# A hybrid decoder step on one core: the inverse's corner blocks brought back by TensorE identity columns, its inputs loaded by two transfers per batch, and four smaller edits

## The chip, the core and the metric

One core of a Trainium2 chip runs the whole kernel. The metric is the device time of one execution in microseconds (us); the time of a kernel is the median of its runs. The kernel before takes 2013.07 us (three runs, 2012.75 to 2020.41).

## What is computed

One layer of a hybrid decoder for 256 prompt tokens and 8 sample tokens, model width 2048, in float32:

```python
x = x + 0.5 * swiglu(rmsnorm(x, n1), f1g, f1u, f1d)      # 2048 -> 5504 -> 2048
h = rmsnorm(x, nm)
proj = h @ w_in                                          # 38 column blocks of 128
o_att, k_buf, v_buf = attend(q, k, v, sinks)             # 16 heads, window 128
o_rwkv, shift, S = rwkv_time_mix(...)                    # 16 heads of 64, matrix state
x = x + concat([o_att, o_rwkv]) @ w_out
x = x + 0.5 * swiglu(rmsnorm(x, n2), f2g, f2u, f2d)
y = rmsnorm(x, final_norm)
# inside rwkv_time_mix, per token and head:
S = S * exp(lw) + (S @ -kk)[..., None] * (kk * a)[None] + v[..., None] * k[None]
y_t = S @ r
```

The kernel does not step through the tokens: it splits the prompt into 4 chunks of 64 and needs, for each head and chunk, the inverse of a triangular 64x64 matrix I + A, which it builds from two 32x32 corner blocks on the diagonal and one block between them.

## The kernel before

All activations lie transposed, 128 features on the partitions by 264 tokens (T = 256 + 8). Every large product is done in a split of float32: a weight chunk of 128x512 (`raw`, 256 KB) is loaded by SP's queue, ScalarE rounds it to `hi` (L123), VectorE forms `lo = raw - hi` (L124), and TensorE multiplies `hi*xh`, `hi*xl` and `lo*xh`: 12 matmuls of 264 columns for one chunk (`gemm`, L127 to L141). Six `raw` and four `hi`/`lo` buffers rotate. The SP queue issues the loads in order and waits, before each, until the buffer it overwrites was read.

There are four phases: the first FFN (`first_ffn`), the mixing (`mixing_body`), and the second FFN (`second_ffn`) with the output scaling at its end; the mixing has the 38 input blocks (`win`), then the output product in three passes over groups of heads (`PASS`).

- The first FFN starts with its x and `vec` (155 columns of gains and other vectors) loaded on ScalarE's queue: `vec` first (L280), then x in pieces of 1, 1, 2, 4, 4 and 4 blocks (L294). `Norm.split` (L164) makes the hi and lo of one block. 14 matmuls on a tile of ones run before the first product (L154).
- In the mixing the side work is written as generators. `prep` makes one pair of heads ready, `chain` does one batch of two pairs (`BATCH`, four batches), `attend` one tile of queries, `dec_attend` the 8 sample tokens' attention. Each chunk of `win` or of the output product calls `tick`, which lets every running generator do one piece; `pause(n)` skips n ticks. `drain` ticks until the generators that a pass needs are done. A scheduler that simulates the engines then places the instructions of each engine in an order of its own; `keep_in_program_order` pins an instruction. At run time every engine and queue works strictly in its order.
- The inverse in `chain` (L517 to L584): `prep` stores the 32x32 corner blocks of its masked products `gm` to a DRAM tile `scr` (tile name `sa`). `chain` loads them twice, as X (each row a whole block, copied to four groups of 32 partitions) and as Y (tile name `Xt`, the rows of the block dealt over the four groups), each by four transfers on SP's queue (L534, L535). After a pause of `DWAIT` ticks, 30 steps of two VectorE operations each (L545, L546) eliminate all corner blocks at once, with the 32 heads, chunks and corners of the batch on the partitions. POOL sets the diagonal. Then Y goes back to a second DRAM tile `scr2` (`sb`, four transfers, L552), after one tick it is read into `TT` with matrix rows on the partitions (four transfers, L557), and after `DWAIT` ticks two VectorE transposes make `TN` (L562). From there on TensorE works: a product of `gm` and `TN` (L569), a copy `zs`, a product of `zs` and `TT` (L580), a copy into `TT`, and the products of `TT` with `KR` that start the chunk chain. X and Y have one buffer each, so a batch's loads wait for the batch before.
- `dec_attend` (L760) multiplies the cached keys by the sample queries (16 products of 8 columns, L775), does the softmax and multiplies the cached values (16 products of 8 columns, L815). Its loads share six buffers `ld`.
- `dec_state` (L298) begins with ten small matmuls that lay out the sample tokens' vectors (XR), in the second FFN.
- At the end VectorE scales the 16 blocks of y by the final root mean square in seven pieces, which SP and ScalarE store in turn (L926, L927).

Of the kernel before, what the change touches and what calls it, by code (L numbers as in the profile page):

```python
# [13 lines left out]
P = 128  # L14
# [15 lines left out]
NS, NO, NY, NH, NT, NLD = 38, 8, 8, 40, 18, 6  # L30
NWARM = 14
NGM, NKR, NUV, NTT, NBT = 10, 5, 3, 2, 5
NSTEP = 4
DWAIT = (8,8,8,4)
# [13 lines left out]
def body(tc, I, O):  # L48
# [46 lines left out]
    with ExitStack() as ctx:  # L95
# [64 lines left out]
        class Norm:  # L160
            def __init__(self, col, most=2):
                self.col, self.most, self.xs, self.sums = col, most, [], [[], []]

            def split(self, x, pin=False, tag="s"):  # L164
                g = vc(self.col + len(self.xs))
                hi, lo = slot(dt=F32R, tag=tag), slot(dt=F32R, tag=tag)
                keep = tc.keep_in_program_order if pin else lambda i: i
                keep(act(hi, x, AF.Copy, scale=g))
                keep(stt(lo, x, g, hi.bitcast(F32), ALU.mult, ALU.subtract))
                self.xs.append((hi, lo))  # L170

# [22 lines left out]
        def early(pi):  # L194
            keep = tc.keep_in_program_order
            if pi == 1:
                keep(A.dma_start(C, I["cst"]))
                keep(A.dma_start(ss, I["shs"]))
# [7 lines left out]
        def ffn(nrm, xr, gu, dn, nxt, load, begin=False, side=None):  # L206
            rstd = None
            f0 = 0
            for pi, nf in enumerate(PARTS):
# [67 lines left out]
        def first_ffn(n2):  # L277
            n1 = Norm(VG1)
            xr = []
            A.dma_start(vec, I["vec"])  # L280
            def load(k0):
                n1.split(xr[k0], k0 >= CH)
# [6 lines left out]
            with tc.tile_pool(name="f1", bufs=1) as fp:  # L289
                cur[0] = (fp, NH)  # L290
                for q in range(4):
                    xg = fp.tile([P, 4, T], F32, tag="x", bufs=4, name=uid("x"))
                    for j in ((0, 1), (1, 2), (2, 4)) if q == 0 else ((0, 4),):
                        A.dma_start(xg[:, j[0]:j[1]], I["xT"][:, q * 4 + j[0]:q * 4 + j[1], :])  # L294
# [32 lines left out]
        def mixing(n2, n3, XD):  # L327
            with tc.tile_pool(name="mx", bufs=1) as mx:
                cur[0] = (mx, NT)
                return mixing_body(mx, n2, n3, XD)  # L330

        def mixing_body(mx, n2, n3, XD):
# [32 lines left out]
            scr2 = [dp.tile([BATCH[b] * 16, 1024], F32, tag=f"sb{b}", name=f"sb{b}") for b in range(nbat)]  # L365
# [156 lines left out]
            def chain(bt):  # L522
# [18 lines left out]
                for s in range(1, 31):  # L541
# [3 lines left out]
                    tt(V, t, bc(X[:, s:s + 1, s + 1:], shp), bc(Y[:, :m, s:s + 1], shp), ALU.mult)  # L545
# [5 lines left out]
                for g in range(ng):  # L551
                    SP.dma_start(scr2[bt.i].rearrange("r (j g t) -> g r j t", g=ng, t=32)[g], Y[g * nr:(g + 1) * nr])  # L552
                yield from pause(1)
                for h in range(2):
                    for blk in range(2):
                        x = h * 64 + blk * 32
                        SP.dma_start(TT[x:x + 32, :, blk * 32:blk * 32 + 32],  # L557
                                     scr2[bt.i].rearrange("(h b m) (s t) -> h b s m t", h=2, b=2, s=32)[h, blk])
                yield from pause(DWAIT[bt.i])
                TN = ring((P, n * 4, 32), "TN", 1)  # L560
                for h in range(2):
                    V.transpose(TN[h * 64:h * 64 + 32], TT[h * 64:h * 64 + 32, :, 0:32])  # L562
# [100 lines left out]
                for k in range(n):  # L663
# [5 lines left out]
                    mixed[p] = o  # L669
                yield  # L670
# [364 lines left out]
```

## Time and profile before

| | us |
|---|---|
| median of 3 runs | 2013.07 |
| the profiled execution, its own time | 2017.98 |
| its span from first to last instruction | 2016.2 |
| TensorE busy in it | 1993.4 |
| VectorE busy | 1307.2 |
| ScalarE busy | 1032.4 |
| GpSimd busy | 255.3 |
| first FFN (to the first product of the mixing) | 0 to some 771 |
| mixing with its output product | some 771 to 1251 |
| second FFN and the output | some 1251 to 2016.2 |

The profile is one execution. PE is TensorE, DVE VectorE, ACT ScalarE, POOL GpSimd; SPq and ACTq are the queues from which transfers are issued. A matmul's rows overlap, so the mean duration of one is longer than the time at which the next starts; busy time divided by the count comes nearer to what one costs. A float32 matmul of the side work (not split) shows as two rows. PEclk is the granted TensorE clock, 1.00 at full rate.

### The profile page before, as it was taken

How to read it: one execution, taken by the hardware profiler on the slowest of the kernel's cores; microseconds unless marked ns; L12 is line 12 of the kernel's file. 1: busy time of each engine (PE TensorE's matmuls, PEld its weight loads, DVE VectorE, ACT ScalarE, POOL GpSimd, SP SyncE). 2: the span in 40 equal slices, each digit the busy share in tenths (PEclk: the TensorE clock that was granted, in tenths of full speed). 3: DMA queues.
4: the chain of work that ended last, by engine and by line, in shares of the span. 5: the costliest groups of instructions: out<-in, count | busy, mean ns of one | idle time of the engine just before them, and what ended most of it. 6: DMA issues, size and time to landing. Idle time of an engine off the chain costs nothing.

```text
span 2016.2 us, 45438 instructions
## 1 busy us (share of the span) xinstructions
PE 1993.4 (99%) x17096; PEld 1960.2 (97%) x17096; DVE 1307.2 (65%) x2577; ACT 1032.4 (51%) x2045; POOL 255.3 (13%) x362
## 2 busy tenths in 40 slices
PE   9999999999999999999999999999999999999998
PEld 9999999999999999999998889999999999999998
DVE  5865555655556577688778756775666666666665
ACT  5644444444444456655555644654444444444445
POOL 0301001010010212122200010120101001010012
PEclk9999999999999999999999989999999999999999
DMA  6666666665656566564555346566666666666654
GB/s 225 177 191 191 185 193 190 184 185 176 186 176 186 181 203 208 155 163 125 141 152 161 114 134 185 176 179 178 191 183 193 183 187 191 188 191 181 197 180 145
DMA packets 227421, 358.38 MB, mean 178 GB/s; under 512 B 42353, under 2 KB 80769, under 8 KB 227201
## 3 DMA queue, kind: packets, MB, share of 16 engines
q1 hardware_dynamic: 220752, 346.95, 58.1%
q10 hardware_dynamic: 6448, 8.53, 1.3%
q8 instruction: 134, 2.20, 0.4%
q14 instruction: 87, 0.70, 0.1%
HBM read 347.25 MB, written 10.21 MB: 177 GB/s over the span
## 4 chain that ended last, share of the span: by engine, by line
PE 94%; DMA 2%; DVE 2%; ACT 1%; issue 1%; SPq 0%; DVEq 0%; ACTq 0%; POOL 0%; POOLq 0%
PE acc L74 86%; PE m L74 8%; DVE lo L58 0%; ACT t L68 0%; DMA TT<-sb 0%; DVE y L58 0%; DMA sb<-Xt 0%; DMA raw<-in_win 0%; DMA ld<-in_cv 0%; DMA raw<-in_gu 0%; PE m L502 0%; DMA sa<-gm 0%; DMA out_vp<-s 0%; DVE st L58 0%; DVE Xt L58 0%
## 5 line engine op out<-in xcount | busy, mean ns | idle before, releaser
L58 DVE TENSOR_TENSOR lo<-raw,hi 128x512 fp32r<-128x512 f32 (+1 forms) x1288 | 870.7, 680 | 548.3 <-ACT hi L123 521.6
L123 ACT CAST hi<-raw 128x512 fp32r<-128x512 f32 (+1 forms) x1288 | 776.8, 607 | 846.6 <-PE acc L74 767.0
L74 PE MATMUL acc<-s,hi 128*128 128x264 f32 x5940 | 1112.6, 286 | 2.1 <-ACT hi L123 1.9
L74 PEld LDWEIGHTS acc<-s,hi 128*128 128x128 f32 x5940 | 925.5, 189 | 8.2 <-ACT hi L123 2.3
L74 PE MATMUL acc<-s,lo 128*128 128x264 f32 x2970 | 848.3, 286 | 1.5 <-DVE lo L58 1.4
L74 PEld LDWEIGHTS acc<-s,lo 128*128 128x128 f32 x2970 | 560.6, 189 | 3.5 <-DVE lo L58 1.9
L74 PE MATMUL acc<-t,hi 128*128 128x264 f32 x2752 | 503.0, 284 | 0.0
L74 PEld LDWEIGHTS acc<-t,hi 128*128 128x128 f32 x2752 | 426.3, 188 | 0.0
L74 PE MATMUL acc<-t,lo 128*128 128x264 f32 x1376 | 388.9, 285 | 0.0
L58 POOL TENSOR_TENSOR t<-t,t 128x264 f32<-128x264 f32 (+1 forms) x148 | 151.0, 1020 | 1149.9 <-ACT hi L123 790.4
L74 PEld LDWEIGHTS acc<-t,lo 128*128 128x128 f32 x1376 | 258.4, 188 | 0.1
L74 PE MATMUL acc<-y,hi 128*128 128x264 f32 x648 | 124.3, 285 | 0.0
L74 PEld LDWEIGHTS acc<-y,hi 128*128 128x128 f32 x648 | 101.1, 188 | 0.2
L74 PE MATMUL acc<-y,lo 128*128 128x264 f32 x324 | 91.7, 283 | 0.0
L58 DVE TENSOR_TENSOR t<-acc,t 128x264 f32<-128x264 f32 x156 | 67.4, 432 | 36.7 <-PE acc L74 36.5
L58 POOL TENSOR_TENSOR o<-o,o 128x264 f32<-128x264 f32 x43 | 36.1, 841 | 231.9 <-ACT o L68 227.9
L74 PE MATMUL acc<-o,hi 128*128 128x264 f32 x324 | 63.0, 284 | 0.0
L74 PEld LDWEIGHTS acc<-y,lo 128*128 128x128 f32 x324 | 60.8, 188 | 0.0
L61 DVE SCALAR_TENSOR_TENSOR s<-acc,s 128x264 f32<-128x264 f32 x96 | 40.7, 428 | 16.0 <-PE acc L74 15.5
L74 PEld LDWEIGHTS acc<-o,hi 128*128 128x128 f32 x324 | 50.3, 188 | 0.0
L74 PE MATMUL m<-s,hi 128*128 128x264 f32 x260 | 48.8, 286 | 0.0
L61 DVE SCALAR_TENSOR_TENSOR x<-acc,x 128x264 f32<-128x264 f32 x96 | 40.6, 427 | 10.0 <-PE acc L74 9.6
(243 smaller groups left out, 1282.7 us busy)
## 6 DMA issues: line engine op xcount, KB each, us to landing
raw<-in_gu SPq DMA_DIRECT2D x688, 256.0 KB, 3.4
raw<-in_dn SPq DMA_DIRECT2D x224, 256.0 KB, 2.8
raw<-in_win SPq DMA_DIRECT2D x152, 256.0 KB, 3.4
raw<-in_dn SPq DMA_DIRECT2D x160, 192.0 KB, 2.7
raw<-in_wout SPq DMA_DIRECT2D x64, 256.0 KB, 3.4
xsp<-x ACTq DMA_DIRECT2D x16, 132.0 KB, 3.6
s<-xsp SPq DMA_DIRECT2D x16, 132.0 KB, 3.8
ld<-in_sT SPq DMA_DIRECT2D x16, 128.0 KB, 3.6
```

The costliest lines, as they stand in the source:

```text
L58: return e.tensor_tensor(out=out, in0=a, in1=b, op=op)
L61: return V.scalar_tensor_tensor(out=out, in0=a, scalar=s, in1=b, op0=op0, op1=op1)
L74: TE.matmul(out, lhsT, rhs, start=start, stop=stop, **k)
L123: A.copy(hi[:, :w], raw[:, :w])
```

## The change

Six things change; the arithmetic stays.

1. The way back of the corner blocks. The eight transfers through `scr2` and the two transposes go. TensorE multiplies each of the eight 32-column slices of Y, as the weights, by columns of the identity (the constant `ident`, tile name `C`) that pick the rows of one head half and one corner: 8 x 2 x 2 = 32 matmuls of 32 columns for each batch, into one PSUM bank. ScalarE copies the bank to `TN`, which now holds both corners, and VectorE transposes the four 32-row groups of `TN` into `TT` (four transposes for a batch instead of two). The pause ahead of it is 8 ticks, where there were 1 and then `DWAIT`.
2. X and Y come by one transfer each instead of four; the first elimination step of a batch is pinned in program order; `DWAIT` of the last batch is 2 instead of 4.
3. The decoder attention's key products become two generators `dec_scores`, one after each four query tiles, with a yield after each four products; the value products yield after each four too.
4. The ten XR matmuls move from the second FFN to the end of the last batch's chain.
5. At the start the gains of the first norm come with the first block of x in one transfer (`x0`), `vec` is loaded in the second part of the FFN, the blocks 4 to 15 of x are asked for one group at a time, the first four splits are pinned and the other banks' chunks are issued behind them; 10 matmuls on ones instead of 14.
6. At the end y is scaled in nine pieces, three of them by GpSimd from a copy of the scale that ScalarE makes.

```diff
@@ -27,11 +27,11 @@
 NACC, NM = 3, 5
-NS, NO, NY, NH, NT, NLD = 38, 8, 8, 40, 18, 6
-NWARM = 14
+NS, NO, NY, NH, NT, NLD = 38, 8, 8, 40, 16, 6
+NWARM = 10
 NGM, NKR, NUV, NTT, NBT = 10, 5, 3, 2, 5
 NSTEP = 4
-DWAIT = (8,8,8,4)
+DWAIT = (8,8,8,2)
 PW = (2, 1, 3, 2, 9)
...
@@ -158,16 +158,19 @@
         class Norm:
-            def __init__(self, col, most=2):
-                self.col, self.most, self.xs, self.sums = col, most, [], [[], []]
+            def __init__(self, col, most=2, gains=None):
+                self.gains = vec[:, col:col + KD] if gains is None else gains
+                self.most, self.xs, self.sums = most, [], [[], []]
 
             def split(self, x, pin=False, tag="s"):
-                g = vc(self.col + len(self.xs))
+                k = len(self.xs)
+                g = self.gains[:, k:k + 1]
                 hi, lo = slot(dt=F32R, tag=tag), slot(dt=F32R, tag=tag)
                 keep = tc.keep_in_program_order if pin else lambda i: i
-                keep(act(hi, x, AF.Copy, scale=g))
+                ins = keep(act(hi, x, AF.Copy, scale=g))
                 keep(stt(lo, x, g, hi.bitcast(F32), ALU.mult, ALU.subtract))
                 self.xs.append((hi, lo))
+                return ins
 
...
@@ -194,6 +197,7 @@
             if pi == 1:
+                keep(A.dma_start(vec, I["vec"]))
                 keep(A.dma_start(C, I["cst"]))
...
@@ -216,11 +220,14 @@
                     for k in range(CH):
-                        load(k)
+                        at = load(k)
                     for k0 in range(0, KD, CH):
+                        if begin and k0 + CH < KD:
+                            begin(k0 // CH + 1)
                         xs = nrm.xs + [None] * (KD - len(nrm.xs))
                         for i, ps in enumerate(banks):
-                            gemm(ps, gu[i // 2, i % 2], xs, rng=(k0,), ahead=False)
+                            with tc.issue_after(at.ins) if begin and k0 == 0 < i else nullcontext():
+                                gemm(ps, gu[i // 2, i % 2], xs, rng=(k0,), ahead=False)
                             if i >= len(banks) - CH and k0 + CH < KD:
...
@@ -275,11 +282,8 @@
         def first_ffn(n2):
-            n1 = Norm(VG1)
-            xr = []
-            A.dma_start(vec, I["vec"])
             def load(k0):
-                n1.split(xr[k0], k0 >= CH)
+                return n1.split(xr[k0], True)
 
...
@@ -288,22 +292,23 @@
                 cur[0] = (fp, NH)
-                for q in range(4):
-                    xg = fp.tile([P, 4, T], F32, tag="x", bufs=4, name=uid("x"))
-                    for j in ((0, 1), (1, 2), (2, 4)) if q == 0 else ((0, 4),):
-                        A.dma_start(xg[:, j[0]:j[1]], I["xT"][:, q * 4 + j[0]:q * 4 + j[1], :])
-                    xr += [xg[:, j] for j in range(4)]
-                ffn(n1, xr, I["gu1"], I["dn1"], nxt, load, True)
-
-        def dec_state(fp, XD):
-            XR = fp.tile([P, 5, 64], F32, name="XR")
-            ps = mp()
-            for i in range(5):
-                for h in range(2):
-                    r = HALF[h]
-                    mm(ps[r, i * 64:i * 64 + 64], XD[r, i, :, :], C[r, CID:CID + P][:, r])
-            A.copy(XR, ps[:, :320].rearrange("p (c t) -> p c t", c=5))
-            yield
+                x0 = fp.tile([P, KD + T], F32, name="x0")
+                A.dma_start(x0, I["x0"])
+                n1 = Norm(VG1, gains=x0[:, 0:KD])
+                xr = [x0[:, KD:]]
+                for j0, j1 in ((1, 2), (2, 4)):
+                    xg = fp.tile([P, j1 - j0, T], F32, name=uid("x"))
+                    A.dma_start(xg, I["xT"][:, j0:j1, :])
+                    xr += [xg[:, j] for j in range(j1 - j0)]
+
+                def more(q):
+                    xg = fp.tile([P, 4, T], F32, tag="x", bufs=3, name=uid("x"))
+                    tc.keep_in_program_order(A.dma_start(xg, I["xT"][:, q * 4:q * 4 + 4, :]))
+                    xr.extend(xg[:, j] for j in range(4))
+
+                ffn(n1, xr, I["gu1"], I["dn1"], nxt, load, more)
+
+        def dec_state(fp, XR):
             n = 4
...
@@ -530,10 +534,8 @@
                 Y = ring((ng * nr, nj, 32), "Xt", 1)
-                for g in range(ng):
-                    SP.dma_start(X[g * nr:(g + 1) * nr], scr[bt.i].rearrange("r (s t) -> r s t", s=32))
-                    SP.dma_start(Y[g * nr:(g + 1) * nr],
-                                 scr[bt.i].rearrange("r (j g t) -> g r j t", g=ng, t=32)[g])
+                SP.dma_start(X.rearrange("p s t -> p (s t)"), bc(scr[bt.i].unsqueeze(0), (ng, nr, 1024)))
+                SP.dma_start(Y, scr[bt.i].rearrange("r (j g t) -> g r j t", g=ng, t=32))
                 TT = ring((P, n * 4, 64), "TT", NTT)
...
@@ -542,24 +544,28 @@
                     shp = (ng * nr, m, w)
-                    tt(V, t, bc(X[:, s:s + 1, s + 1:], shp), bc(Y[:, :m, s:s + 1], shp), ALU.mult)
+                    keep = tc.keep_in_program_order if s == 1 else lambda i: i
+                    keep(tt(V, t, bc(X[:, s:s + 1, s + 1:], shp), bc(Y[:, :m, s:s + 1], shp), ALU.mult))
                     tt(V, Y[:, :m, s + 1:], Y[:, :m, s + 1:], t, ALU.add)
...
                     G.memset(Y[g * nr:(g + 1) * nr].rearrange("p j t -> p (j t)")[:, g:g + (nj - 1) * (32 + ng) + 1:32 + ng], 1.0)
-                for g in range(ng):
-                    SP.dma_start(scr2[bt.i].rearrange("r (j g t) -> g r j t", g=ng, t=32)[g], Y[g * nr:(g + 1) * nr])
-                yield from pause(1)
-                for h in range(2):
+                yield from pause(8)
+                ps = mp()
+                cols = ident[:, :ng * nr].rearrange("p (g h b m) -> p g h b m", g=ng, h=2, b=2)
+                for j in range(nj):
                     for blk in range(2):
+                        for h in range(2):
+                            x = h * 64 + blk * 32
+                            mm(ps[x:x + 32, j * ng * n * 4:(j + 1) * ng * n * 4], Y[:, j, :], cols[:ng * nr, :, h, blk, :])
+                TN = ring((P, n * 4, 32), "TN", 1)
+                A.copy(TN, ps[:, :32 * n * 4].rearrange("p (s m) -> p m s", m=n * 4))
+                yield
+                for blk in range(2):
+                    for h in range(2):
                         x = h * 64 + blk * 32
-                        SP.dma_start(TT[x:x + 32, :, blk * 32:blk * 32 + 32],
-                                     scr2[bt.i].rearrange("(h b m) (s t) -> h b s m t", h=2, b=2, s=32)[h, blk])
-                yield from pause(DWAIT[bt.i])
-                TN = ring((P, n * 4, 32), "TN", 1)
-                for h in range(2):
-                    V.transpose(TN[h * 64:h * 64 + 32], TT[h * 64:h * 64 + 32, :, 0:32])
+                        V.transpose(TT[x:x + 32, :, blk * 32:blk * 32 + 32], TN[x:x + 32])
                 yield
...
@@ -667,6 +673,13 @@
                     mixed[p] = o
+                if len(bts) == nbat and bt is bts[-1]:
+                    ps = mp()
+                    for i in range(5):
+                        for h in range(2):
+                            r = HALF[h]
+                            mm(ps[r, i * 64:i * 64 + 64], XD[r, i, :, :], ident[r, r])
+                    A.copy(XR, ps[:, :320].rearrange("p (c t) -> p c t", c=5))
                 yield
...
@@ -757,24 +770,30 @@
 
-            def dec_attend(att):
-                yield
-                qb = tmp((P, 2, NB, 2, 4))
+            sd = fix((P, P), "sd")
+
+            def dec_scores(p):
+                yield
+                qb = tmp((P, NB, 2, 4))
                 G.memset(qb, 0.0)
...
                     r = HALF[h]
-                    G.tensor_copy(qb[r, :, :, h, :], qd[r])
+                    G.tensor_copy(qb[r, :, h, :], qd[r, p])
                 yield
                 sps = mp()
-                sv = sps[:, :P].rearrange("p (h x) -> p h x", h=2)
-                for p in range(2):
-                    for b in range(0, NB, 2):
-                        kc = load(I["kc"][p, b // 2], (P, 2, P))
-                        for j in range(2):
-                            c0 = p * 32 + (b + j) * 4
-                            mm(sv[:, :, c0:c0 + 4], kc[:, j, :], qb[:, p, b + j])
-                st = tmp((P, P))
-                A.copy(st, sps[:, :P])
+                sv = sps[:, :64].rearrange("p (h x) -> p h x", h=2)
+                for b in range(0, NB, 2):
+                    kc = load(I["kc"][p, b // 2], (P, 2, P))
+                    for j in range(2):
+                        mm(sv[:, :, (b + j) * 4:(b + j) * 4 + 4], kc[:, j, :], qb[:, b + j])
+                    if b % 4 == 2:
+                        yield
+                A.copy(sd.rearrange("p (h x) -> p h x", h=2)[:, :, p * 32:p * 32 + 32], sv)
+
+            def dec_attend(att, scores):
+                while any(g in tasks for g in scores):
+                    yield
+                st = sd
                 pr = tmp((P, 2, NB, 4))
...
@@ -813,6 +832,8 @@
                         mm(ov[:, :, c0:c0 + 4], vcache[:, p * P:(p + 1) * P], pv[:, :, c0:c0 + 4])
+                    if b % 2:
+                        yield
                 of = od.rearrange("p a b i -> p (a b i)")
...
@@ -853,8 +874,10 @@
                     att.append(spawn(attend(i, q)))
+                    if i % 4 == 3:
+                        scores.append(spawn(dec_scores(i // 4)))
                     if len(att) == 8:
-                        att.append(spawn(dec_attend(list(att))))
+                        att.append(spawn(dec_attend(list(att), scores)))
             n2.xs = None
...
@@ -921,9 +944,12 @@
                     mm(rp[:, j * 88:j * 88 + 88], bc(rt[:, j:j + 1], (88, P)), C[0:88, CID:CID + 88])
-                for i, (o, n) in enumerate(((0, 1), (1, 1), (2, 2), (4, 4), (8, 4), (12, 2), (14, 2))):
+                rb = tmp()
+                A.copy(rb, rp[:, :T])
+                for i, (e, o, n) in enumerate(((V, 0, 1), (V, 1, 1), (G, 2, 1), (V, 4, 4), (G, 3, 1), (V, 8, 4), (G, 14, 1), (V, 12, 2), (V, 15, 1))):
                     y = ys[o // 4][:, o % 4:o % 4 + n]
-                    tt(V, y, y, bc(rp[:, :T].unsqueeze(1), (P, n, T)), ALU.mult)
+                    r = rb if e is G else rp[:, :T]
+                    tt(e, y, y, bc(r.unsqueeze(1), (P, n, T)), ALU.mult)
                     (SP, A)[i % 2].dma_start(O["yT"][:, o:o + n, :], y)
...
@@ -969,6 +996,7 @@
         a[f"dn{n}"] = c(i[f"ffn{n}_w_down"][0].reshape(NF, P, KD, P).transpose(2, 1, 0, 3).reshape(KD, P, FF))
+    a["x0"] = c(np.concatenate([i["ffn1_norm"][0].reshape(KD, P).T, a["xT"][:, 0]], 1))
     cols = _sources()
...
     rows = np.concatenate([1024 + k * P + np.arange(P) if k < 8 else _qcols(k - 8) for ks in PASS for k in ks])
```

More of the change, by code (lines that the diff above doesn't have):

```diff
@@ L204, in copy_one, with ffn @@
             tc.keep_in_program_order(A.dma_start(O[n][b, 0:127, :], I[c][b, 1:128, :]))
-        def ffn(nrm, xr, gu, dn, nxt, load, begin=False, side=None):
+        def ffn(nrm, xr, gu, dn, nxt, load, begin=None, side=None):
             rstd = None
@@ L325, in dec_state, with mixing, mixing_body @@
                 SP.dma_start(O["wkvs"][:, r, :], S)
-        def mixing(n2, n3, XD):
+        def mixing(n2, n3, XD, XR):
             with tc.tile_pool(name="mx", bufs=1) as mx:
                 cur[0] = (mx, NT)
-                return mixing_body(mx, n2, n3, XD)
-        def mixing_body(mx, n2, n3, XD):
+                return mixing_body(mx, n2, n3, XD, XR)
+        def mixing_body(mx, n2, n3, XD, XR):
             def fix(shape, name):
@@ L364, in mixing_body @@
             scr = [dp.tile([BATCH[b] * 16, 1024], F32, tag=f"sa{b}", name=f"sa{b}") for b in range(nbat)]
-            scr2 = [dp.tile([BATCH[b] * 16, 1024], F32, tag=f"sb{b}", name=f"sb{b}") for b in range(nbat)]
             mixed = [None] * 16
@@ L829, in mixing_body @@
             ts(G, sgl, sgl, 0.5, ALU.mult, 0.5, ALU.add)
-            bat, att, bts = [], [], []
+            bat, att, bts, scores = [], [], [], []
             for kind, i in SEQ:
@@ L888, in mixing_body, with second_ffn @@
             return xr
-        def second_ffn(n3, xr, XD):
+        def second_ffn(n3, xr, XR):
             fin = Norm(VGF, 3)
@@ L906, in nxt @@
                     act(ys[o // 4][:, o % 4], xr[o], AF.Copy, scale=vc(VGF + o))
-                side = dec_state(fp, XD)
-                ffn(n3, xr, I["gu2"], I["dn2"], nxt, load, False, side)
+                side = dec_state(fp, XR)
+                ffn(n3, xr, I["gu2"], I["dn2"], nxt, load, None, side)
                 assert next(side, side) is side
@@ L933, in body @@
             XD = dx.tile([P, 8, NPAIR, NB], F32, name="XD")
-            second_ffn(n3, mixing(n2, n3, XD), XD)
+            XR = dx.tile([P, 5, 64], F32, name="XR")
+            second_ffn(n3, mixing(n2, n3, XD, XR), XR)
 OUTS = dict(yT=(P, KD, T), kp=(2, P, P), vp=(2, P, P), ks=(NB, P, 256), vs=(NB, P, 256),
```

## The prediction

> **What bounds the kernel now.** I read the page's engine table first, then the chain that ended last, then busy time by stretches of the span, and last the waits and groups inside the mixing.
>
> ```profile
> PE 1993.4 (99%) x17096; PEld 1960.2 (97%) x17096; DVE 1307.2 (65%) x2577; ACT 1032.4 (51%) x2045; POOL 255.3 (13%) x362
> PE 94%; DMA 2%; DVE 2%; ACT 1%; issue 1%; SPq 0%; DVEq 0%; ACTq 0%; POOL 0%; POOLq 0%
> ```
> ```profile
> 200.00:700.00 500.00, 500.00 (x4113) 500.00 (x4112) 286.64 (x488) 236.10 (x417) 53.16 (x50) 1.00 0.61 184
> 760.00:1260.00 500.00, 489.85 (x4776) 458.69 (x4775) 365.38 (x967) 284.60 (x695) 70.31 (x168) 0.98 0.54 154
> ```
>
> TensorE is the bound and carries 94% of the chain. In the steady first FFN (columns: stretch, its length, then busy time and count of PE, PEld, DVE, ACT, POOL, then the granted clock) it runs without a gap at 500/4113 = 0.1216 us a matmul. Nothing is to be won there. In the mixing it is idle for 500 - 489.85 = 10.15 us, and its clock falls. The next rows show where: five stretches chosen around the gaps, then four in which the clock was halved.
>
> ```profile
> 900.00:912.00 12.00, 9.90 (x93) 9.03 (x93) 2.73 (x5) 5.03 (x11) 1.04 (x4) 0.86 0.70 173
> 1036.00:1040.00 4.00, 2.58 (x22) 2.38 (x21) 2.76 (x7) 0.49 (x2) 0.19 (x1) 1.00 0.34 90
> 1090.00:1106.00 16.00, 13.56 (x153) 11.98 (x152) 11.63 (x44) 12.86 (x43) 1.33 (x2) 0.79 0.88 257
> 1165.00:1178.00 13.00, 13.00 (x90) 12.56 (x88) 5.87 (x18) 6.02 (x21) 0.00 (x0) 0.74 0.52 150
> 1187.00:1198.00 11.00, 9.35 (x62) 7.72 (x62) 3.76 (x11) 3.97 (x11) 3.30 (x10) 0.84 0.26 70
> ```
> ```profile
> 906.43:909.84 3.41, 3.41 (x41) 3.35 (x42) 1.20 (x2) 1.28 (x4) 1.04 (x4) 0.50 0.58 158
> 1097.57:1104.40 6.83, 6.67 (x73) 5.75 (x73) 5.04 (x27) 5.54 (x21) 0.74 (x1) 0.50 0.95 296
> 1169.25:1176.08 6.83, 6.83 (x33) 6.83 (x32) 2.24 (x7) 2.75 (x7) 0.00 (x0) 0.50 0.58 167
> 1193.15:1196.56 3.41, 3.41 (x14) 2.25 (x14) 1.08 (x3) 1.43 (x5) 2.35 (x6) 0.50 0.28 77
> ```
>
> The reader is to see 20.48 us at half rate, so 10.2 us lost beside the 10.15 us idle: some 20.4 us is all that waiting costs in the mixing. The rest of it is work.
>
> **What the removed way back costs now.** VectorE works in order, and the `lo` of later weight chunks stands behind its waits (who waited, on what: sum, times, longest):
>
> ```profile
> DVE TN L562 <- DMA TT<-sb: 11.5, 6, 3.5
> DVE st L58 <- DMA Xt<-sa: 8.5, 2, 4.5
> DVE st L58 <- DMA out_vp<-s: 4.3, 1, 4.3
> DVE st L58 <- DMA raw<-in_win: 3.2, 1, 3.2
> ```
> ```profile
> 906.36 1.03 PE L74 MATMUL m<-TN,gm 32*32 32x32 f32 x30 [0.99 <-DVE TN L562]
> L552 SPq DMA_DIRECT2D sb<-Xt x16: 550/570/1369, 895.5 to 1087.0; - x16
> ```
>
> The transposes wait 11.5 us for the second DRAM trip, the first elimination steps 8.5 + 4.3 + 3.2 = 16.0 us for X and Y. Most of it is covered by the four `lo` buffers (4 x 12 x 0.1216 = 5.8 us of matmuls). Where it isn't, TensorE shows it: the stretch at 900 (12 - 9.90 = 2.1 idle, and 3.41 at half rate, 1.7) and the one at 1036 (1.4, a `lo` behind a transpose). These 3.8 + 1.4 = 5.2 us go: in the new way TN,gm needs only ScalarE's copy, and in the order in which the built kernel's instructions stand some 3 us of other matmuls stand between the identity products and TN,gm in each batch. SP loses 55 issues, the 16 at 0.57 us of the row above among them, so raw loads come earlier; X and Y become fewer, larger ones.
>
> **What it adds on TensorE.** 4 batches x 32 float32 matmuls, two rows each: 256 rows of 128 rows high, 32 columns wide, 32 moving columns. No row of before has that form. The nearest, with busy time:
>
> ```profile
> L74 PE MATMUL m<-TN,gm 32*32 32x32 f32 x128 | 3.6, 203 | 2.2 <-DVE TN L562 2.1
> L74 PE MATMUL m<-uv,BT 128*64 128x64 f32 x128 | 4.9, 226 | 0.4 <-ACT uv L599 0.4
> L74 PE MATMUL m<-t,ld 128*128 128x8 f32 x64 | 8.3, 263 | 1.6 <-DMA ld<-in_cv 1.6
> ```
> ```profile
> 982.03 0.69 PE L74 MATMUL m<-TT,zs 32*32 32x32 f32 x32
> 982.65 0.39 PE L74 MATMUL acc<-s,lo 128*128 128x264 f32 x1
> ```
>
> TN,gm has the width and the moving size: 3.6/128 = 28 ns a row. uv,BT is as high, with twice the width: 38 ns. Full width costs 8.3/64 = 130 ns. The least is 32 rows from 982.03 to 982.65, 19 ns each. I take 28 ns, since the width agrees: 256 x 0.028 = 7.2 us, all on the bounding engine. Ends: 5.0 us (19 ns) and, far out, 33.3 us (130 ns); the likely end is 9.7 us (38 ns). The Trainium skill, TensorEngine Tiling (Array Packing), Tiling Modes, speaks against the change here: switching the tiling mode drains TensorE. The two timeline rows show a switch into and out of such a mode in 0.62 us with all 32 rows in it, so a drain is small; at an estimated 0.1 us a switch the eight new ones would make 0.8 us, and the sum 2006.8.
>
> **What it adds elsewhere.** Eight more VectorE transposes, four more ScalarE copies from PSUM:
>
> ```profile
> L562 DVE STREAM_TRANSPOSE TN<-TT x8: 432/434/436, 902.9 to 1094.2; 32x256 f32<-32x256 f32 x8
> L748 ACT COPY t<-m 128x256 f32<-128x256 f32 x16 | 5.7, 371 | 5.5 <-PE m L747 5.4
> ```
>
> 8 x 0.434 = 3.5 us of VectorE, which the 27.5 us of waits above pay for, and 4 x 0.371 us = 1.5 of ScalarE. If that cover is gone, four times 0.87 us (two transposes) stand ahead of a `lo`: 3.5 us, the upper end. Behind the pinned first step wait `lo` chunks; in batch two Y is issued three raw loads behind X, so that wait stays. I put 0.8 us of new idle time on TensorE (0 to 3.5).
>
> **The attention's products.** Before the half rate at 1169 stands this row:
>
> ```profile
> 1166.01 2.74 PE L74 MATMUL m<-t,ld 128*128 128x8 f32 x24
> ```
>
> TensorE was never idle in 1165 to 1178, yet the clock halved right after 24 rows of 8 columns. The change cuts this run into groups of eight rows with work between (built order), so I let the 6.83/2 = 3.4 us go. The Trainium skill, TensorE: Matmul & The Clock Gate, part 1, ties half rate to an idle window of some 3.4 us; the steps of 3.41 and 6.83 us agree, the idle window isn't in the trace. The value products go the other way: they now stand as 32 rows with small matmuls only between, where 24 and 8 stood; the stretch at 1187 (1.65 idle, 1.7 by clock) stays, and I add 1.0 us (0 to 1.7) for a longer half rate. In the last batch TN,gm, the zs products and the queries' softmax collide on ScalarE: 1090 to 1106 lost 2.44 idle and 6.83/2 = 3.4. In the new order 41 chunk matmuls (41 x 0.1216 = 5.0 us) stand between TN,gm and the zs products, more than the wait: I let the 5.9 us go (0 to 5.9). The ten XR matmuls cost the same in either place.
>
> **Start and end.**
>
> ```profile
> 0.73 0.42 ACTq L280 DMA_DIRECT2D vec<-in_vec  x1
> 1.25 1.34 ACTq L294 DMA_DIRECT2D x<-in_xT  x3
> 7.24 0.51 ACT L68 ACTIVATE s<-x,vec 128x264 fp32r<-128x264 f32 x1 [4.56 <-DMA raw<-in_gu]
> 8.40:12.20 3.80, 3.80 (x17) 3.58 (x18) 3.60 (x7) 2.65 (x6) 0.00 (x0) 0.55 1.03 396
> L58 DVE TENSOR_TENSOR y<-y,m x7: 422/699/1249, 2007.3 to 2011.5; 128x528 f32<-128x528 f32 x3, 128x264 f32<-128x264 f32 x2, 128x1056 f32<-128x1056 f32 x2
> L58 POOL TENSOR_TENSOR o<-o,o 128x264 f32<-128x264 f32 x43 | 36.1, 841 | 231.9 <-ACT o L68 227.9 <-PE acc L74 2.3 <-issue 1.7
> ```
>
> The first split starts at 7.24; its two inputs were issued at 0.73 and 1.25. As one transfer in the first place it can start up to the 0.9 us earlier that issue and queue cost, but the next three splits (3 x 0.51 us) now stand ahead of the second `hi`. The 3.8 us at clock 0.55 lose 1.7 us, which fewer warming matmuls may keep, double or save. I take -1.0 us (-2.6 to +1.5). At the end two scalings of 0.70 leave VectorE and one of 0.42 comes: -0.98; GpSimd's three (3 x 0.84 = 2.5 us, behind a copy) end within VectorE's remaining 4. The stores still have to drain: -0.6 us (-1.0 to +0.5).
>
> **The sum.** -5.2 - 3.4 - 5.9 + 7.2 + 0.8 + 1.0 - 1.0 - 0.6 = -7.1 us. The profiled execution took 2017.98 (span 2016.2), so 2010.9 under the profiler; it stands 4.9 above the median, 2013.07, so the forecast is 2006.0.
>
> **Rivals.**
> - B, all waiting goes: VectorE, relieved of 27.5 us of waits, keeps ahead everywhere. For it: 20.4 us is there, 14.5 counted; against: gaps remain that wait for ScalarE. 5.9 more, no longer value run (1.0), best start and end (1.6 + 0.4): 1997.1.
> - R, the half rate at 1169 has another cause than the narrow run: its 3.4 us stay, 2009.4. For it: only one such run is seen; against: it is followed at once. The rule of the Trainium skill, TensorE: Matmul & The Clock Gate, that is weighed above would lead here.
> - C, the waits move: attention and the last chain collide in another place, 5.9 + 3.4 stay: 2015.3. For it: two more table loads on ScalarE in that stage; against: the wider spacing.
> - D, slower: the identity products cost what 128-row, full-width ones cost, 130 ns: 33.3 in place of 7.2, 2032.1. For it: equal height; against: the weights are 32 wide, and uv,BT, as high, costs 38. Above 7.2 + 7.1 = 14.3 us, 56 ns a row, the change loses.
> - E, VectorE held at the pinned step: transfers four times as large take twice the 4.5 us wait, 9; beyond 5.8 us of cover TensorE idles 3.2 and loses 1.7 by clock, four times: +19.6, 2025.6. Against: in three batches the loads are issued earlier relative to the step than before.
>
> **How the numbers follow.** The forecast gets 0.42 (own range 2000 to 2011), B 0.24, R 0.06, C 0.14, D 0.08, E 0.06. About 0.5% (10 us) is what a measurement here can tell from no change. Faster than 2003: B and three tenths of the forecast, 0.37; slower than 2023: D, E and a little of C, 0.16; between 0.47. The range from 1995 to 2019 leaves out D, E and the edges of B and C.
>
> **What would show it.** The group m<-C,Xt with 256 rows near 7 us busy; no VectorE wait for sb; clock 1.00 after the first half of the mixing; one half-rate stretch near the value products; 0.1216 us a matmul elsewhere. A busy time of that group above 14 us, or more than 15 us idle plus half rate in the mixing, would prove me wrong.

## The result, and the profile after

The changed kernel takes 2025.08 us (median of 6 runs, 2020.82 to 2028.70) beside 2014.35 us for the kernel before on the same chip (6 runs, 2012.15 to 2020.41): a ratio of 1.0048, 95% interval 1.0035 to 1.0060. It is slower by 10.7 us in the medians, where 7 us of gain were forecast, and lies outside the predicted range (1995 to 2019). The profiled execution took 2025.33 us (span 2023.5).

The first view is the page of the kernel after: busy time of each engine, then the chain that ended last, by engine and by line.

```profile
PE 1992.9 (98%) x17344; PEld 1961.4 (97%) x17344; DVE 1312.0 (65%) x2584; ACT 1037.1 (51%) x2053; POOL 257.3 (13%) x368
PE 95%; DMA 2%; DVE 1%; ACT 1%; issue 0%; SPq 0%; ACTq 0%; DVEq 0%; POOL 0%
PE acc L74 86%; PE m L74 9%; DMA Xt<-sa 2%; DMA sa<-gm 0%; DVE lo L58 0%; DMA x<-in_xT 0%; DVE y L58 0%; DVE st L58 0%; DVE Xt L58 0%; PE m L506 0%; SPq L487 0%; ACT L68 0%; PE m L758 0%; ACT t L68 0%; PE m L759 0%
```

TensorE is still the bound, with the same busy time although it got 256 rows more; the span grew by 7.3 us. The landing of Y (`Xt<-sa`) now makes 2% of the chain. By stretches (length, then busy time and count of PE, PEld, DVE, ACT, POOL, clock, DMA share, GB/s) the mixing shows where the time went, and the three stretches that the prediction let go follow:

```profile
200.00:700.00 500.00, 500.00 (x4114) 500.00 (x4113) 286.71 (x488) 235.99 (x418) 53.03 (x50) 1.00 0.59 184
760.00:1260.00 500.00, 481.70 (x4971) 451.92 (x4971) 364.95 (x966) 283.95 (x694) 69.44 (x170) 0.97 0.49 148
900.00:912.00 12.00, 11.69 (x162) 10.42 (x156) 2.25 (x10) 5.85 (x14) 1.26 (x4) 1.00 0.30 75
1036.00:1040.00 4.00, 4.00 (x35) 4.00 (x34) 3.84 (x8) 3.41 (x11) 0.98 (x3) 1.00 0.37 112
1090.00:1106.00 16.00, 16.00 (x188) 13.96 (x188) 14.44 (x41) 9.17 (x23) 0.66 (x1) 1.00 0.50 149
```

The first FFN is as it was. The stretches at 900, 1036 and 1090 are full, but for 0.31 us in the first, and at clock 1.00, as forecast, yet TensorE's idle time from 760 to 1260 rose from 10.15 to 500 - 481.70 = 18.30 us. It is mostly idle in three other places, and the clock halves in or right behind each of them; the fourth halved stretch stands near the value products. The next rows are the four:

```profile
915.60:922.43 6.83, 4.58 (x82) 4.47 (x84) 6.58 (x22) 2.43 (x9) 1.88 (x6) 0.50 0.26 81
990.70:997.53 6.83, 2.98 (x52) 2.86 (x54) 6.43 (x21) 2.54 (x8) 0.64 (x3) 0.50 0.40 112
1065.80:1072.63 6.83, 5.28 (x90) 4.98 (x92) 6.34 (x26) 2.86 (x8) 0.73 (x1) 0.50 0.47 135
1188.70:1195.53 6.83, 6.83 (x32) 6.28 (x31) 3.10 (x7) 2.30 (x6) 2.80 (x10) 0.50 0.02 8
```

Half of the busy time in them is lost: (4.58 + 2.98 + 5.28 + 6.83)/2 = 9.8 us, so 28.1 us of idle time and half rate together, where before had 20.3 by the same count (and where above 15 was to prove the prediction wrong). The waits of VectorE from 840 to 1110, of ScalarE there, and of TensorE in the whole span (who waited, on what: sum, times, longest) give the path:

```profile
DVE st L58 <- DMA Xt<-sa: 31.0, 3, 12.2
```
```profile
ACT uv L605 <- DVE uv L605: 20.4, 5, 9.2
```
```profile
PE m L74 <- ACT W L603: 15.1, 4, 6.8
PE acc L74 <- DVE lo L58: 2.1, 2, 1.9
```

and one of the three places in order of time, first from the chain that ended last (start, duration, what), then from the timeline (in brackets the idle time ahead and what ended it):

```profile
978.19 10.44 DMA Xt<-sa
```
```profile
988.73 0.19 DVE L58 TENSOR_TENSOR st<-X,Xt 128x30 f32<-128x30 f32 x1 [12.20 <-DMA Xt<-sa]
993.35 0.41 DVE L605 COPY uv<-m 64x256 f32<-64x256 f32 x1
993.79 0.37 ACT L605 COPY uv<-m 64x256 f32<-64x256 f32 x1 [9.23 <-DVE uv L605]
994.18 0.32 ACT L603 COPY W<-m 128x192 f32<-128x192 f32 x1
994.55 0.48 PE L74 MATMUL m<-BT,W 64*64 64x64 f32 x4 [6.83 <-ACT W L603]
```

Y is issued at 978.19 and lands 10.44 us later. VectorE stands at the first step, pinned, for 12.20 us. The copy `uv` of the chunk chain stands behind it and some of the steps; ScalarE's copies `uv` and `W` stand behind that, and TensorE needs `W` for the next product of the chain. It is idle for 6.83 us and then runs at half rate. This is rival E of the prediction, its place right, its chance put at 0.06. That its price, 2025.6, is so near is luck: it is 2006.0 + 19.6, and the runs below put the two parts at 2009.46 (e4) and 15.6.

Why Y lands so late is seen while X's transfer runs almost alone (after, three batches; the last two columns are the DMA share and GB/s):

```profile
845.00:849.50 4.50, 4.50 (x36) 4.42 (x35) 1.93 (x3) 2.76 (x6) 0.52 (x1) 1.00 0.25 74
980.00:985.00 5.00, 5.00 (x68) 4.65 (x62) 0.00 (x0) 2.29 (x5) 0.00 (x0) 1.00 0.26 87
1055.00:1060.00 5.00, 5.00 (x83) 4.80 (x84) 0.00 (x0) 1.25 (x4) 0.00 (x0) 1.00 0.27 84
```

A quarter of the 16 DMA engines is busy, and 512 KB at 74 GB/s take 7.1 us. X's access begins with a dimension of four (the four copies); in the first batch its packets run from 843.5 to 850.9, and Y's, 3.2 us of them, only then. Y's access begins with a dimension of four as well, and while its packets run alone a quarter of the engines is busy again (the kernel after):

```profile
851.50:853.00 1.50, 1.50 (x15) 1.50 (x14) 0.07 (x1) 0.91 (x3) 0.00 (x0) 1.00 0.26 41
```

In the kernel before each of X's four transfers begins with 32 rows. The view of transfers from 830 to 1100 has them (count, KB each, median us from issue to landing):

```profile
X<-sa SPq DMA_DIRECT2D x16, 128.0 KB, 3.0
```

The Trainium skill has the rule in DMA: Bandwidth & Descriptors, Why a DMA increments its semaphore by 16 and not by 1: a transfer uses as many engines as the largest number up to 16 that divides the slowest dimension of more than one element in both of its access patterns. Rules for kernel authors, on that page of the Trainium skill, warns of a leading broadcast of c copies. The share of 0.25 agrees with four engines of 16.

### The profile page after: what moved, and what is told of

Its sections match the earlier page's. It is cut to its first block, busy times and chain, and to the rows that moved or that the text cites. A ratio compares the mean times of both kernels' runs of the same rounds, so it can differ in the third digit from the quotient of the medians.

```text
span 2023.5 us, 45884 instructions
## 1 busy us (share of the span) xinstructions
PE 1992.9 (98%) x17344; PEld 1961.4 (97%) x17344; DVE 1312.0 (65%) x2584; ACT 1037.1 (51%) x2053; POOL 257.3 (13%) x368
## 4 chain that ended last, share of the span: by engine, by line
PE 95%; DMA 2%; DVE 1%; ACT 1%; issue 0%; SPq 0%; ACTq 0%; DVEq 0%; POOL 0%
PE acc L74 86%; PE m L74 9%; DMA Xt<-sa 2%; DMA sa<-gm 0%; DVE lo L58 0%; DMA x<-in_xT 0%; DVE y L58 0%; DVE st L58 0%; DVE Xt L58 0%; PE m L506 0%; SPq L487 0%; ACT L68 0%; PE m L758 0%; ACT t L68 0%; PE m L759 0%
```

## The experiments

Thirteen kernels were run, each beside the kernel before on the same chip. Ratios are to that, with 95% intervals.

| kernel | us, median (runs) | ratio to before |
|---|---|---|
| the changed kernel | 2025.08 (6) | 1.0048 (1.0035 to 1.0060) |
| e1: X and Y by four transfers each | 2017.15 (10) | 1.0011 (1.0001 to 1.0021) |
| e2: no pin | 2032.47 (4) | 1.0092 (1.0068 to 1.0115) |
| e3: X by one, Y by four | 2026.70 (4) | 1.0057 (1.0036 to 1.0079) |
| e4: X by four, Y by one | 2009.46 (8) | 0.9970 (0.9959 to 0.9981) |
| e5: before, with X and Y by one each | 2036.00 (4) | 1.0100 (1.0085 to 1.0116) |
| e6: Y issued ahead of X | 2027.85 (4) | 1.0057 (1.0042 to 1.0072) |
| e7: later first step | 2020.39 (10) | 1.0016 (1.0006 to 1.0025) |
| e8: X by four, old way back, no pin | 2014.88 (10) | 0.9997 (0.9988 to 1.0007) |
| e9: X by four, no pin | 2010.36 (9) | 0.9977 (0.9965 to 0.9990) |
| e10: before, with the new way back, pin, Y by one | 2009.46 (5) | 0.9970 (0.9957 to 0.9983) |
| e11: e4 with Y first and other pauses | 2002.44 (4) | 0.9941 (0.9921 to 0.9960) |
| e12: Y first, two buffers for Y | 2015.54 (10) | 1.0000 (0.9990 to 1.0009) |
| e13: X by two transfers | 2043.71 (4) | 1.0130 (1.0114 to 1.0147) |

### Which part is slow: e1 to e4

e1 has both loads by four transfers, as before:

```diff
-                SP.dma_start(X.rearrange("p s t -> p (s t)"), bc(scr[bt.i].unsqueeze(0), (ng, nr, 1024)))
-                SP.dma_start(Y, scr[bt.i].rearrange("r (j g t) -> g r j t", g=ng, t=32))
+                for g in range(ng):
+                    SP.dma_start(X[g * nr:(g + 1) * nr], scr[bt.i].rearrange("r (s t) -> r s t", s=32))
+                    SP.dma_start(Y[g * nr:(g + 1) * nr],
+                                 scr[bt.i].rearrange("r (j g t) -> g r j t", g=ng, t=32)[g])
```

> The changed kernel with X and Y loaded by four transfers each, as before; the pin of the first step, the identity products and all else as in the changed kernel. Theory T (the merged transfers land late, some 10 us after their issue, and VectorE stands at the first elimination step): VectorE's waits for Xt fall from 31 us in three to under 10, TensorE's waits for the copy W fall from 15 us to under 3, and the time to 2002 to 2010, under that of the kernel before. Theory P (the pin holds the step too early): waits and time stay, above 2018. Theory M (something else of the change costs it, such as the identity products): above 2018 with the waits gone.

e2 leaves both by one transfer and takes the pin away:

```diff
-                    keep = tc.keep_in_program_order if s == 1 else lambda i: i
+                    keep = lambda i: i
```

> The changed kernel without the pin of the first step; X and Y still by one transfer each. T: the transfers land as late as before, the step waits wherever it stands among VectorE's instructions: 2017 to 2032, VectorE's waits for Xt over 20 us. P: under 2012, waits under 10 us.

e3 takes only Y by four, e4 only X by four:

> The changed kernel with Y by four transfers and X still by one. T, in the form that one X transfer takes some 7 us because its outermost run of four is spread over few engines: waits of 5 to 9 us a batch, 2012 to 2024. If Y alone were the late one: 2002 to 2010, as with four and four.

> The changed kernel with X by four transfers and Y still by one. T in the form that X is the slow one: Y lands in some 5 to 6 us instead of 10, 2004 to 2014. If Y's 1024 small rows alone were the late ones: above 2018.

The four medians are 2017.15, 2032.47, 2026.70 and 2009.46. X by one transfer is the loss: e4 differs from the changed kernel only in X and is 15.6 us faster; e3, which merges only X, is as slow as the changed kernel. That is slower than the 2012 to 2024 expected of e3: Y's four transfers land as late behind X as the one did (VectorE waits 22.1 us for Xt in two waits, the longest 13.4). The pin isn't the cause: without it the time is 7 us worse, half a microsecond above the range expected. e1 gains 7.9 us but misses the 2002 to 2010 that it was to reach: its eight issues alternate X and Y, and the last of them land late again. The waits of VectorE from 840 to 1110 in e4 and then in e1:

```profile
DVE st L58 <- DMA Xt<-sa: 14.4, 3, 6.5
```
```profile
DVE st L58 <- DMA raw<-in_win: 10.6, 2, 7.4
DVE st L58 <- DMA Xt<-sa: 7.9, 1, 7.9
```

The first step reads only X and Y; the two waits of e1 that the view puts down to `raw` end 0.3 and 0.4 us after a Y and an X landed. In e4 the wait fell from 31.0 to 14.4 us. So Y by one transfer, five issues a batch instead of eight, is a gain: 2009.46 beside 2017.15.

### The merged loads alone: e5

The kernel before, with the two lines that e1 takes out put in:

> The kernel before with one edit: X and Y by one transfer each. Theory (X's one transfer takes some 7 us, Y's comes behind it, and VectorE stands at the first elimination step with uv and lo behind it): slower than before by 8 to 25 us (2022 to 2040), a VectorE wait of st for Xt of over 9 us in at least three batches. Rival (the loss belongs to the pinned step or to the new way back, the larger transfers alone are harmless or spare SP six issues a batch): 2008 to 2018.

It is slower than before by 20 us, more than the whole change, and a wait of `st` for Xt stands in all four batches, over 9 us in two of them, where at least three were expected (waits of VectorE from 840 to 1110, and the stretch 760 to 1260):

```profile
DVE st L58 <- DMA Xt<-sa: 37.0, 4, 13.0
```
```profile
760.00:1260.00 500.00, 476.45 (x4649) 445.36 (x4648) 357.55 (x951) 275.81 (x682) 68.67 (x168) 0.97 0.50 148
```

TensorE is idle 23.55 us there, and 27.3 us long at half rate. The rival, that larger transfers are harmless by themselves, falls. What the rest of the change is worth follows: 2036.00 to 2025.08, some 11 us of gain.

### Order and place: e6 and e7

e6 issues Y ahead of X, both merged; e7 leaves the loads and lets the first step come later:

```diff
-DWAIT = (8,8,8,2)
+DWAIT = (14,14,14,4)
```

> The changed kernel with Y's transfer issued ahead of X's. If both share the few DMA engines on which X's transfer was seen (DMA share 0.25 while it ran), the later of the two lands as late as before: 2021 to 2029, VectorE's longest wait at st still 9 to 13 us. Rival (the order matters: Y's small packets run beside X's on other engines, or X's 7 us alone is what is late): waits shorter by some 3 us in each batch, 2010 to 2019.

> The changed kernel with DWAIT (14,14,14,4) in place of (8,8,8,2): both loads stay one transfer each, the first step stands some five chunks (7 us) later behind its loads in the first two batches, two to three chunks in the third, and no later in the last. Theory (only the landing is late): the VectorE waits at st fall below 6 us in the first three batches, 2010 to 2019. Rival (the merged transfers cost by themselves, by what they take from the raw loads, or the chain that follows is what is short of time): 2021 to 2030.

e6 took 2027.85 us: the order does nothing, the later of the two lands as late (VectorE now waits 29.2 us for X and 10.1 for Y). In e7 the waits for Xt fall to 9.1 us, of which 1.7 in the first three batches, as the theory said, and 7.4 in the last, whose pause grew least; but the time falls only to 2020.39 us, between both ranges: inconclusive on the time. TensorE's waits show what is late next (e7, whole span):

```profile
PE m L74 <- DVE st L58: 3.7, 1, 3.7
PE m L74 <- POOL t L58: 3.6, 2, 2.7
PE acc L74 <- DVE lo L58: 2.4, 1, 2.4
PE m L74 <- DVE Xt L58: 1.7, 2, 1.5
```

The steps now stand so late that TensorE waits for them (the rows with `st` and `Xt`). There isn't room for a load of 10 us ahead of the steps: as far as these two pauses show: held early it blocks VectorE, held late the chain starts late.

### The other parts: e8, e9 and e10

e8 is e4 with the way back through `scr2` as before, without the pin and with `DWAIT` (8,8,8,4); e9 is e4 without the pin; e10 is the kernel before with the new way back, the pin, `DWAIT` (8,8,8,2) and Y by one transfer.

> The changed kernel with X by four transfers and Y by one, the way back of the corner blocks through DRAM as before, no pin, DWAIT (8,8,8,4). What it has over the same kernel with the identity products and no pin (not yet run; some 2009 to 2014) is the price of the old way back. By the prediction's terms (5.2 us of stalls and the 5.9 us at 1090 come back, the identity products' 2.8 us of TensorE leave): 2015 to 2021. If the old way back cost nothing: 2007 to 2013.

> The changed kernel with X by four transfers, Y by one, and no pin. Against the same with the pin (2009.5): if the pin earns what it did with both merged (some 7 us), 2013 to 2018; if the pin only matters while VectorE stands long at the step, 2008 to 2012. Against the same with the old way back (2014.9, ratio 0.9997): the difference is the price of the old way back; by the prediction some 5 to 11 us, so 2004 to 2010; if the old way back was nearly hidden, 2012 to 2016.

> The kernel before with only the way back by identity columns, the pinned first step, DWAIT (8,8,8,2) and Y by one transfer; X by four, attention, XR, start and end as before. If the way back (with its pin) is what gained in the version at 2009.5 and the other four edits are worth 1 us together, as the kernel with the old way back says: 2007 to 2013 beside some 2014.5. By the prediction's terms (way back 5.2, its products 2.8, the stretch at 1090 counted with the attention's spacing): 2009 to 2014. If the gain needs the other edits: 2013 to 2018. The half rate that follows the key products should be there again (some 6.8 us near 1165), which it isn't in the changed kernel.

e8 beside e9, 2014.88 and 2010.36 (0.9997 and 0.9977): the old way back costs some 4 us more than the new one. That is an estimate from two intervals that just overlap, and each time lies between the two ranges named for it, so the price is between what the prediction's terms gave and nothing. The pin is worth about 1 us here (e4 and e9, the intervals overlap) against 7 with the slow X, which fits a pin that matters only while VectorE stands long at the step. e10 is as fast as e4: the way back, its pin and Y by one transfer are the whole gain, 5 to 6 us; the attention, XR, start and end edits are together worth nothing that these runs can tell. In e10 the key products stand as one run again, and the clock halves behind them, though for half as long as expected (timeline, then the halved stretch):

```profile
1157.91 2.74 PE L74 MATMUL m<-t,ld 128*128 128x8 f32 x24
```
```profile
1161.80:1165.20 3.40, 3.40 (x18) 3.40 (x17) 1.43 (x4) 0.62 (x1) 0.00 (x0) 0.50 0.50 160
```

Not every such run is followed by a halved clock. The value products of e10 and then of e5, which also keeps the old attention, stand as one run of 24 rows too, and behind them the clock stays at 1.00:

```profile
1177.68 2.74 PE L74 MATMUL m<-t,ld 128*128 128x8 f32 x24
1177.60:1190.00 12.40, 12.40 (x96) 10.39 (x96) 6.56 (x16) 5.87 (x16) 4.62 (x12) 1.00 0.32 97
```
```profile
1201.74 2.74 PE L74 MATMUL m<-t,ld 128*128 128x8 f32 x24
1201.70:1214.00 12.30, 12.30 (x98) 10.51 (x96) 6.44 (x16) 5.52 (x15) 4.43 (x11) 1.00 0.34 99
```

### Shape or size: e13

X by two transfers of two groups each, the rest as in the changed kernel:

```diff
-                SP.dma_start(X.rearrange("p s t -> p (s t)"), bc(scr[bt.i].unsqueeze(0), (ng, nr, 1024)))
+                for g in range(0, ng, 2):
+                    SP.dma_start(X[g * nr:(g + 2) * nr].rearrange("p s t -> p (s t)"), bc(scr[bt.i].unsqueeze(0), (2, nr, 1024)))
```

> The changed kernel with X by two transfers of two groups each (256 KB, outermost dimension 2), Y by one. Theory of the shape (a transfer runs on as many DMA engines as its outermost dimension has rows): two engines for each transfer, so X takes as long as in one transfer if the two fall on different engines (some 7 us, DMA share 0.25, time 2021 to 2029) or twice as long if they fall on the same two (14 us, share 0.13, 2035 to 2060). Theory of the size (a transfer of 512 KB is slow because it is large; half of it takes half as long): X lands in some 3.5 us, DMA share above 0.3, 2008 to 2016.

2043.71 us, the shape's second case. While X runs nearly alone (e13; DMA share and GB/s last):

```profile
852.00:855.00 3.00, 3.00 (x27) 3.00 (x26) 0.67 (x2) 1.26 (x5) 0.00 (x0) 1.00 0.13 53
1074.00:1083.00 9.00, 5.12 (x57) 4.60 (x56) 0.00 (x0) 0.05 (x1) 0.00 (x0) 1.00 0.14 49
```

The share is 0.13 to 0.14, two engines of 16: both halves of X go to the same two, and with half the size the load runs not faster but slower, at 49 to 53 GB/s against 74 to 87. The size theory (faster, share above 0.3) falls. VectorE waits 50.2 us for Xt, the longest 15.2. The Trainium skill, DMA: Bandwidth & Descriptors, Why a DMA increments its semaphore by 16 and not by 1, names the lowest-numbered engines for this kind of queue. The share agrees: had each transfer taken its own two, the share would have been 0.25.

### A faster version: e11 and e12

e11 is e4 with Y's transfer ahead of X's four and `DWAIT` (8,9,10,3); e12 is e4 with Y ahead and two buffers for Y, for which the attention's small loads have five (`NLD`) instead of six.

> The changed kernel with Y's one transfer issued ahead of X's four wherever its buffer allows, DWAIT (8,9,10,3). If the landing of Y behind X is what still holds VectorE at 2009.5 (14.4 us in three waits): waits for Xt or X below 8 us together, 2003 to 2008. If X then lands as late as Y did, or what is left is no wait for a load: 2008 to 2013.

> The changed kernel with Y's one transfer ahead of X's four and two buffers for Y (five in place of six for the small attention loads), so that Y's load no longer waits for the identity products of the batch before. If that buffer is what makes the second batch's load late: 2002 to 2008. If X's landing decides, or the attention misses its sixth load buffer: 2008 to 2014.

e11 beats both kernels: 2002.44 us, 0.9941 of before (0.9921 to 0.9960). Its mixing (760 to 1260):

```profile
760.00:1260.00 500.00, 492.15 (x5090) 462.08 (x5090) 372.47 (x981) 292.60 (x710) 69.72 (x170) 0.99 0.51 153
```

7.85 us idle and 6.83 us long at half rate. The waits of `st` for a load are 9.2 us for Xt and 4.3 for X, hardly less than the 14.4 of e4 and above the 8 that the theory expected, and the time lies just below the 2003 to 2008 expected. What made it faster than e4 isn't settled: order and pauses changed together, the four runs lie between 2001.68 and 2008.89, and the profiled one is the slowest of them. e12 misses: the second buffer lets Y go early, and X now lands last (VectorE waits 21.5 us for X, 8.5 at most); 2015.54 us lies above both ranges.

## Why the prediction was wrong

The step that failed is the end of "What it adds elsewhere": "I put 0.8 us of new idle time on TensorE (0 to 3.5)", and with it the sentence against rival E, that the loads are issued earlier in three batches. The merged loads were counted as issues saved on SP ("X and Y become fewer, larger ones") and their landing as unchanged. Nothing in the profile of before said how long a transfer of that form takes. Its cost needed a bound of its own, and the bound went by the wait of the kernel before. In place of the 0.8 us, VectorE waited 31.0 us for Y and TensorE 15.1 us for `W` behind it, and idle time and half rate in the mixing grew from 20.3 to 28.1 us where they were to fall. The shape of the access was in the diff: a leading four. Seven us for X and three for Y behind it outlast the 5.8 us of cover, which E had worked out. E had the cause of the delay wrong: it went by the size, and e13, with half the size and longer waits, shows that the shape decides.

- The way back (5.2 us): right. No wait for `sb` is left, the stretches at 900 and 1036 are full, and e9 beside e8 gives some 4 us with the products paid.
- The identity products (7.2 us): mis-sized. The group of the kernel after reads

```profile
L74 PE MATMUL m<-C,Xt 128*32 128x32 f32 x256 | 3.1, 199 | 0.0
```

  3.1/256 = 12 ns a row, below the lower end of 19. Neighbouring rows go to different groups of 32 columns and start some 7 ns apart in the trace (median); that the groups are the reason no run tests. D falls.
- The stretch at 1090 (5.9 us): right, as its row shows; C falls.
- The key products (3.4 us): the half rate is gone, but its cause is open. Behind the groups of eight no profile has it. Of the five runs of 24 such rows in the profiles of before, e5 and e10, only two have it right behind them, the key products of before and of e10; behind the value products it is missing in e5 and e10, and in before it comes 5 us later, after an idle wait of 1.65 us. The prediction called the run at 1166 the only one and overlooked the one at 1185. So a narrow run alone doesn't halve the clock, and the premise of R, another cause, stands, though its price doesn't show. The Trainium skill, TensorE: Matmul & The Clock Gate, part 1, asks for an idle window. Ahead of both halvings TensorE is busy without a gap (14.20 of 14.20 us before, 13.80 of 13.80 in e10), so the rule as stated doesn't cover them.
- The value products (1.0 us): the half rate near them is 6.83 us long in the kernel after, 3.41 before, 1.7 us more, at the end of the range given. It is no fixed price: with the same edit it is 6.83 us long in e4, e7, e9 and e11, 3.41 in e3, and missing in the other six. In the kernel after, the spacing of the attention earns 3.4 us and loses 1.7.
- XR (nothing): from the 8700th to the 11000th of the chunk matmuls, counted in the trace, before and e10 take 282.7 us, the kernel after and e4 280.9, so the place that they left is 1.8 us shorter. What they cost in the new place no run measures, and e10 beside e4 shows no gain of the whole.
- The start (1.0 us): the first product comes at 6.1 instead of 8.3 us, but the clock then halves from 7.7 for 6.83 us; by the 480th chunk matmul 0.2 us are left (68.8, 69.0). In e4, with the same start, it halves for 3.41 us and 1.0 us is left (68.0); the range given covers both. The end (0.6 us): nothing; from the 14900th chunk matmul to the end of the span 22.1 us pass, 22.0 before.

The sum without the merged X came out near: e4 stands 5.0 us below before, 7.1 were forecast. That is partly luck: the identity products cost 4.1 us less than counted, while e4 still has 5.5 us of idle time on TensorE for `W` and 6.83 us at half rate behind it, where the sum had 0.8. With the merged X, what the new way back saved was lost again, and more, to the wait of 31.0 us on VectorE.

## What to carry to other kernels

Before several transfers are merged into one, read the first dimension of the merged access: four there put 512 KB on a quarter of the DMA engines, and two transfers beginning with two put it on an eighth. The size counts beside the shape: Y by one transfer ran on a quarter too, but its 128 KB land in some 3 us, and with X by four its merging was a gain (2009.46 beside 2017.15). A load that an in-order engine waits for is priced by its landing, not by its issues; what stands behind the waiting instruction says what the delay costs, and here the copy of another chain did. When a term rests on "lands as before", give it both ends from its own shape.

## What was not expected of the hardware

- The share of the DMA engines followed the leading dimension: 0.25 to 0.27 for four, 0.13 to 0.14 for two, and two such transfers in flight didn't add up.
- 12 ns of TensorE's time for a float32 row of 128 x 32 weights and 32 columns, when neighbouring rows use different column groups, against 28 ns for 32 x 32 tiles in the kernel before.
- A halved clock behind 24 rows of 8 columns with TensorE busy throughout, for 6.83 us in the kernel before and 3.41 in e10, but not right behind three other runs of the same form. What decides isn't shown.
